# A two-layer attention and convolution trunk on one core: four edits around the end of attention jobs

## The chip, the cores and the metric

The kernel runs on one core of one Trainium2 chip. The metric is the device time of one execution in microseconds (us); of the kernel before, three runs are shown with their median. One further execution was profiled, and all rows below come from it. Its engines are named PE (TensorE matmul), PEld (weight load of PE, beside it), DVE (VectorE), ACT (ScalarE), POOL (GpSimd) and SP (SyncE, here only a queue that issues DMAs). Times in rows are counted from the start of the span.

## The reference, cut to what matters

Two layers; in each, 2048 latent tokens and 256 context tokens pass an input projection, eight-head attention, two convolution branches and an output projection:

```python
def one_block(qi):
    s = jnp.einsum('bqhd,bkhd->bhqk', qi, k).astype(jnp.float32) * sm_scale
    p = jax.nn.softmax(s, axis=-1).astype(v.dtype)
    return jnp.einsum('bhqk,bkhd->bqhd', p, v)
...
y = mixer_branches(parts, attn, ...)            # y_a = attn * silu(g_a), and two more branches
x_new = x + gate[:, None, :] * (y @ w_out[l])
```

All is float32. Latent queries see 256 + 2048 keys; context queries see the 256 context keys, and only in the first layer.

## The kernel before, in words

**Stages.** Per layer the program runs `tokens`, `features`, `attention` and `project`. In the profile the attention of layer 0 lies at about 815 to 1790 us, its projection at 1762 to about 1970, the attention of layer 1 at about 2640 to 3557, its projection from 3544 to the end.

**Attention jobs.** A job is one head and 512 queries; there are 32 per layer, in order of heads, and in layer 0 the last job of each head also carries 256 context queries. A job goes through its 18 key tiles in 9 pairs (one more pair for the context queries). For one pair PE makes two scores tiles `sc` in three matmuls each (L1074 to L1076), ACT takes the exponential twice, as `p` in float32 and `ph` in a reduced form (L1077, L1078), one `tensor_tensor` subtracts them to the rest `pl` (L1081), and one pair later PE multiplies `ph` and `pl` with the values into `po` (L1103, L1104). DVE adds `p` to the row sums `acc` in PSUM (L1088). Beside that PE computes for the next job all its scores once more as `pmax` (L986), whose maxima DVE reduces to `mx` (L987). `pmax` has two PSUM buffers (tag "b"), so PE waits there once DVE is two tiles late; `p` has four buffers.

**The end of a job** is `close` (L1109 to L1120, called by `flush` behind the products of the last pair): ACT copies `acc` to `accs` (L1108) and `po` to `o` (L1110), SP stores `o`, PE transposes `accs` in four pieces (L1116), DVE adds along the rows (L1118: `sm`), doubles the sums (L1119), and takes the reciprocal into `rinv` (L1120). The factor 2 makes up for the gate, which is stored at twice its value (as x times 1 + tanh(x/2)).

**The last job of a layer.** It has no next job, hence no `pmax` beside most of it. There DVE takes the subtraction L1081 of every odd pair (five instructions in layer 0, four in layer 1); POOL has all the others.

**Projection.** `project` splits each of eight weight blocks (128 x 1024) into `woh` (ACT, L191) and `wol` (DVE, L192) by way of one buffer `wraw`, and each block of 512 tokens into `yh` and `yl`. For the four parts k of attention output, `prepare_y` loads the two halves `yr` and `ylo` and the gate `yg`, spreads the reciprocals `rinv` over 128 columns in four small tiles `rr` (L1178), transposes these on PE into `prr` (L1179), and DVE makes sum, product and product (L1180 to L1182). Then PE has 24 matmuls per output tile (`pout`, L195 to L197). `rr` has three buffers. `prr` of the first block uses the PSUM tag "b" of `pmax`; weights 0 to 2, 3, and 4 to 7 lie in three pools whose memory comes free with tiles of attention.

**Order.** The framework orders each engine's instructions at build time by priority and a simulated timeline; on the chip every engine works its list in order. `attention` returns a mark: the priority at a given number of pairs (`AE`) before the end of the last job. What `project` issues under `start()` (weights 0 to 3 and the first block's `prepare_y`) gets the priority of that mark.

Of the kernel before, what the change touches and what calls it, by code (L numbers as in the profile page):

```python
# [9 lines left out]
F32 = mybir.dt.float32  # L10
F32R = mybir.dt.float32r
I32 = mybir.dt.int32
AF = mybir.ActivationFunctionType
ALU = mybir.AluOpType
# [4 lines left out]
P = 128  # L19
# [30 lines left out]
MV = 0  # L50
MD = 2
NE = 2
PV = 0
AE = 2
WM = (0,0,0,1,2,2,2,2)
SPV = 7
ZF = 4
# [28 lines left out]
def trunk(ctx: ExitStack, tc: tile.TileContext, ins, out):  # L86
    nc = tc.nc
    V, S, G, PE = nc.vector, nc.scalar, nc.gpsimd, nc.tensor

    def pool(stack, name, **kw):  # L90
        return stack.enter_context(tc.tile_pool(name=name, bufs=kw.pop("bufs", 1), **kw))
# [9 lines left out]
    rinv = [cst.tile([P, NTT, H], F32, name=f"rinv{l}") for l in range(DEPTH)]  # L101
# [838 lines left out]
    def attention(l, start):  # L940
# [3 lines left out]
        op = pool(es, f"Ao{l}", reuse_waits="tile", side="right")  # L944
# [4 lines left out]
        jobs = []  # L949
# [6 lines left out]
        scale = QK ** -0.5  # L956
# [3 lines left out]
        def load(h):  # L960
            K = hp[h % 2].tile([97, NTT, 2, P], F32R, tag="K", name="K")
            G.dma_start(K[0:NOPE], kn_d[l][h])
            G.dma_start(K[NOPE:97], kr_d[l][h])
            Q = hp[h % 2].tile([97, NTT, 2, P], F32R, tag="Q", name="Q")
            nq_ = (SEQ if last else NT) // P
            G.dma_start(Q[0:QK, :nq_], q_d[l][h, :, :nq_])
            Vt = vp.tile([P, NTT, P], F32R, tag=f"V{h % 2}", name="Vt")
            G.dma_start(Vt, v_d[l][h])
            kv[h] = (K, Vt, Q)
# [84 lines left out]
        for idx, job in enumerate(jobs):  # L1054
            h = job[0][0]
            if job[0][1] == (1024 if h else 512) and h + 1 < H:
                load(h + 1)
            pairs = [(j, it) for j in job for it in range(j[3], NTT, 2)]
            for pi, ((h, s, n, k0), kt0) in enumerate(pairs):
                if idx == len(jobs) - 1 and pi == len(pairs) - AE:  # L1060
                    mark = tc.cur_priority
                K, Vt, Q = kv[h]
                first, final = kt0 == k0, kt0 == NTT - 2
                if first:
                    po = psum("c", "po")
                    acc = psum("d", "acc")
                p = tp.tile([P, 2, 512], F32, tag="p", name="p", bufs=4)
                ph = tp.tile([P, 2, 512], F32R, tag="ph", name="ph", bufs=3)
                pl = tp.tile([P, 2, 512], F32R, tag="pl", name="pl", bufs=3)
                scs = []  # L1070
                for z in range(2):
                    kt, qt = kt0 + z, slice(s // P, (s + n) // P)
                    sc = psum("a", "sc")
                    PE.matmul(sc[:, :n], lhsT=K[0:97, kt, 0], rhs=Q[0:97, qt, 0], start=True, stop=False)  # L1074
                    PE.matmul(sc[:, :n], lhsT=K[0:QK, kt, 0], rhs=Q[0:QK, qt, 1], start=False, stop=False)  # L1075
                    PE.matmul(sc[:, :n], lhsT=K[0:QK, kt, 1], rhs=Q[0:QK, qt, 0], start=False, stop=True)  # L1076
                    S.activation(p[:, z, :n], sc[:, :n], AF.Exp, scale=scale)  # L1077
                    S.activation(ph[:, z, :n], sc[:, :n], AF.Exp, scale=scale)  # L1078

                by = V if idx == len(jobs) - 1 and pi % 2 and pi > PV else G  # L1080
                by.tensor_tensor(pl[:, :, :n], p[:, :, :n], ph[:, :, :n].bitcast(F32), op=ALU.subtract)  # L1081
                flush()

                for z in range(2):
                    if first and z == 0:
                        V.tensor_copy(acc[:, :n], p[:, 0, :n])
                    else:
                        V.tensor_tensor(acc[:, :n], acc[:, :n], p[:, z, :n], op=ALU.add)  # L1088
                for z in range(2):
                    at = pi + (z + 1) / 2 + LEAD  # L1090
                    if at <= len(pairs):
                        ahead(idx + 1, at / len(pairs))
                    else:
                        ahead(idx + 1, 1)
                        ahead(idx + 2, (at - len(pairs)) / len(pairs))
                if pi == len(pairs) // 2:
                    split_mods()
                if pi == len(pairs) - ME:
                    use_mods()

                def products(kt0=kt0, n=n, Vt=Vt, ph=ph, pl=pl, po=po, first=first, final=final):
                    for z in range(2):
                        PE.matmul(po[:, :n], lhsT=Vt[:, kt0 + z, :], rhs=ph[:, z, :n], start=first and z == 0, stop=False)  # L1103
                        PE.matmul(po[:, :n], lhsT=Vt[:, kt0 + z, :], rhs=pl[:, z, :n], start=False, stop=final and z == 1)  # L1104

                def close(h=h, s=s, n=n, po=po, acc=acc):
                    accs = op.tile([P, 512], F32, tag="o", name="accs", bufs=3)
                    S.copy(accs[:, :n], acc[:, :n])  # L1108
                    o = op.tile([P, 512], F32, tag="o", name="o", bufs=3)  # L1109
                    S.copy(o[:, :n], po[:, :n])  # L1110
                    nc.sync.dma_start(o_d[l][h, :, s : s + n], o[:, :n])

                    nq = n // P
                    px = psum("e", "psum_t")
                    for t in range(nq):
                        PE.transpose(out=px[:, t * P : (t + 1) * P], in_=accs[:, t * P : (t + 1) * P], identity=idn)  # L1116
                    sm = tp.tile([P, 4], F32, tag="sm", name="sm", bufs=2)
                    V.tensor_reduce(sm[:, :nq], px[:, :n].rearrange("p (t k) -> p t k", k=P), axis=AX.X, op=ALU.add)  # L1118
                    V.tensor_scalar(sm[:, :nq], sm[:, :nq], 2.0, None, op0=ALU.mult)  # L1119
                    V.reciprocal(rinv[l][:, s // P : s // P + nq, h], sm[:, :nq])  # L1120

                late.append(products)
                if final:
                    late.append(close)
        if not AE:
            mark = tc.cur_priority
# [8 lines left out]
    def project(l, start):  # L1135
# [3 lines left out]
        op = pool(es, f"Oo{l}", reuse_waits="tile", side="right")  # L1139
# [18 lines left out]
        def prepare_y(bi):  # L1158
            s, n = blocks[bi]
            where = (ap, bp)[bi % 2]  # L1160
            yh = where.tile([P, KD, 512], F32R, tag="yh", name="yh")[:, :, :n]
            yl = where.tile([P, KD, 512], F32R, tag="yl", name="yl")[:, :, :n]
            ys[bi] = (yh, yl)
            for k in order:
                r = rp.tile([P, 512], F32, tag="yr", name="yr", bufs=4)
                if k >= 4:
                    nc.sync.dma_start(r[:, :n], y_d[l][(k - 4) * P : (k - 3) * P, s : s + n])
                else:
                    lo = rp.tile([P, 512], F32, tag="ylo", name="ylo", bufs=2)
                    g = rp.tile([P, 512], F32, tag="yg", name="yg", bufs=2)  # L1170
                    for z in range(2):
                        nc.sync.dma_start(r[64 * z : 64 * z + 64, :n], o_d[l][2 * k + z, 0:64, s : s + n])
                        nc.sync.dma_start(lo[64 * z : 64 * z + 64, :n], o_d[l][2 * k + z, 64:128, s : s + n])
                    nc.sync.dma_start(g[:, :n], sga_d[l][k * P : (k + 1) * P, s : s + n])
                    px = psum("b" if bi == 0 else "cde"[k % 3], "prr")
                    for t in range(n // P):
                        rr = rp.tile([P, 2, 64], F32, tag="rr", name="rr", bufs=RR)
                        V.tensor_copy(rr, rinv[l][:, s // P + t, 2 * k : 2 * k + 2].unsqueeze(2).to_broadcast([P, 2, 64]))  # L1178
                        PE.transpose(out=px[:, t * P : (t + 1) * P], in_=rr.rearrange("p a b -> p (a b)"), identity=idn)  # L1179
                    V.tensor_tensor(r[:, :n], r[:, :n], lo[:, :n], op=ALU.add)  # L1180
                    V.tensor_tensor(r[:, :n], px[:, :n], r[:, :n], op=ALU.mult)
                    V.tensor_tensor(r[:, :n], r[:, :n], g[:, :n], op=ALU.mult)  # L1182
                split(yh[:, k, :n], yl[:, k, :n], r[:, :n], V if bi == 0 and (SPV & 4 and k < 4 or SPV & 8 and k >= 4) else None)
                yield
# [9 lines left out]
        for bi, (s, n) in enumerate(blocks):  # L1194
# [4 lines left out]
            acc = None if last else rp.tile([P, 512], F32, tag="acc", name="acc")  # L1199
# [114 lines left out]
```

## Time and profile before

| | |
|---|---|
| runs | 3740.6 us median of three (3739.18 to 3740.98) |
| profiled execution | 3738.87 us, span 3737.1 us |
| PE, PEld | 3543.0 us (95%), 2920.5 us (78%) |
| DVE | 3004.7 us (80%) |
| ACT, POOL | 2143.5 us (57%), 2324.0 us (62%) |
| mean granted clock of PE | 0.975 of full |

The span is read by stage. PE is busy for most of it in every stage, so what counts is where PE stands idle and where its granted clock is at 0.5 (1.2 GHz) in place of 1.0 (2.4 GHz), and which engine it waits for there.

### The profile page before, as it was taken

The page shows a single profiled execution, that of the slowest core. Times are in us where ns is not written, and L with a number is a line of the kernel's source. Part 1 is how long each engine was busy: PE and PEld are TensorE (multiplying, and loading weights), DVE is VectorE, ACT ScalarE, POOL GpSimd, SP SyncE. Part 2 cuts the span into 40 slices and gives each one's busy share as a digit, 9 for nine tenths or more (in the row PEclk, how much of TensorE's full clock was granted, in tenths as well). Part 3 has the DMA queues.
Part 4 walks back from the last instruction along what each step waited for, and adds up shares of the span by engine and source line. Part 5 has one row for each costly group of instructions (what it writes and reads, how often), then busy time and mean ns, then how long its engine had stood idle before and what let it go on. Part 6 is the DMA issues. An engine that isn't in the chain of part 4 may idle for free. (4 is left out here: it accounts for less than half of the span.)

```text
span 3737.1 us, 52826 instructions
## 1 busy us (share of the span) xinstructions
PE 3543.0 (95%) x17532; PEld 2920.5 (78%) x17532; DVE 3004.7 (80%) x5689; ACT 2143.5 (57%) x4192; POOL 2324.0 (62%) x1488
## 2 busy tenths in 40 slices
PE   7889999999999999988999989999999999998999
PEld 5787888887777787777788878887777777776777
DVE  6986886878888888899447878769998999999942
ACT  4665343247777777766335663433677777777610
POOL 4664444358888888875435654444687877877521
PEclk8899999999999999999999999999999999999999
DMA  7566334441333313312666773435222202222163
GB/s 216 171 187 200 88 104 118 109 128 48 85 80 78 78 36 77 79 58 59 220 218 212 216 214 102 117 101 129 77 69 61 45 22 61 58 58 76 40 197 114
DMA packets 394387, 411.48 MB, mean 110 GB/s; under 512 B 19168, under 2 KB 332128, under 8 KB 388960
## 3 DMA queue, kind: packets, MB, share of 16 engines
q1 hardware_dynamic: 387712, 333.87, 30.7%
q0 software_dynamic: 6400, 74.22, 8.8%
q8 instruction: 138, 2.26, 0.3%
q14 instruction: 137, 1.12, 0.1%
HBM read 266.72 MB, written 141.59 MB: 109 GB/s over the span
## 5 line engine op out<-in xcount | busy, mean ns | idle before, releaser
L1081 POOL TENSOR_TENSOR pl<-p,ph 128x1024 fp32r<-128x1024 f32 (+1 forms) x575 | 1365.1, 2391 | 322.5 <-ACT ph L1078 163.9
L987 DVE TENSOR_REDUCE mx<-pmax 128x1 fp32r<-128x512 f32 (+1 forms) x1296 | 794.8, 628 | 98.3 <-PE pmax L986 92.6
L1077 ACT ACTIVATE p<-sc 128x512 f32<-128x512 f32 x1168 | 708.6, 608 | 287.8 <-PE sc L1076 269.3
L1088 DVE TENSOR_TENSOR acc<-acc,p 128x512 f32<-128x512 f32 x1096 | 756.2, 690 | 45.6 <-ACT p L1077 20.2
L1078 ACT ACTIVATE ph<-sc 128x512 fp32r<-128x512 f32 x1168 | 698.2, 607 | 18.3 <-PE po L1103 13.3
L195 PE MATMUL pf<-hhf,wh 128*128 128x256 f32 (+1 forms) x1584 | 547.5, 347 | 14.1 <-ACT wh L191 7.0
L197 PE MATMUL pf<-hhf,wl 128*128 128x512 f32 (+1 forms) x1584 | 544.5, 345 | 5.6 <-POOL wl L192 5.4
L196 PE MATMUL pf<-hlf,wh 128*128 128x256 f32 (+1 forms) x1584 | 546.2, 345 | 0.0
L986 PE MATMUL pmax<-K,Q 96*128 96x512 f32 (+1 forms) x1296 | 474.3, 389 | 57.1 <-DVE mx L987 48.7
L1074 PE MATMUL sc<-Q,K 97*128 97x512 f32 x1168 | 478.8, 410 | 4.3 <-ACT Q L996 1.5
L1104 PE MATMUL po<-pl,Vt 128*128 128x512 f32 x1168 | 468.8, 402 | 5.6 <-DVE pl L1081 5.1
L1075 PE MATMUL sc<-Q,K 96*128 96x512 f32 x1168 | 467.3, 400 | 0.0
L1076 PE MATMUL sc<-Q,K 96*128 96x512 f32 x1168 | 465.0, 398 | 0.0
L1103 PE MATMUL po<-ph,Vt 128*128 128x512 f32 x1168 | 462.0, 396 | 0.7 <-DMA Vt<-v_d 0.7
L192 POOL TENSOR_TENSOR wl<-wraw,wh 128x1024 fp32r<-128x1024 f32 x104 | 254.3, 2446 | 284.7 <-ACT wh L191 267.2
L748 DVE SCALAR_TENSOR_TENSOR cacc<-z,hv,cacc 128x384 f32<-128x384 f32 (+5 forms) x780 | 403.6, 564 | 14.3 <-ACT cacc L743 11.2
L986 PEld LDWEIGHTS pmax<-K,Q 96*128 96x128 f32 x1296 | 246.2, 190 | 152.7 <-DVE mx L987 94.6
L195 PEld LDWEIGHTS pf<-hhf,wh 128*128 128x128 f32 x1584 | 302.7, 191 | 52.9 <-ACT wh L191 9.2
L197 PEld LDWEIGHTS pf<-hhf,wl 128*128 128x128 f32 x1584 | 301.8, 191 | 45.9 <-POOL wl L192 9.2
L196 PEld LDWEIGHTS pf<-hlf,wh 128*128 128x128 f32 x1584 | 303.0, 191 | 36.0 <-POOL hlf L192 0.2
L1074 PEld LDWEIGHTS sc<-Q,K 97*128 97x128 f32 x1168 | 223.6, 191 | 61.6 <-ACT ph L1078 9.6
L1104 PEld LDWEIGHTS po<-pl,Vt 128*128 128x128 f32 x1168 | 222.9, 191 | 56.8 <-DVE pl L1081 6.4
(259 smaller groups left out, 6304.1 us busy)
## 6 DMA issues: line engine op xcount, KB each, us to landing
wraw<-in_w_in SPq DMA_DIRECT2D x108, 512.0 KB
q_d<-sg SPq DMA_DIRECT2D x68, 384.0 KB
wm<-in_w_mod SPq DMA_DIRECT2D x46, 512.0 KB
v_d<-vs SPq DMA_DIRECT2D x36, 512.0 KB
kn_d<-sg SPq DMA_DIRECT2D x72, 256.0 KB
K<-kn_d POOLq DMA_DIRECT2D x16, 1152.0 KB, 8.5
Vt<-v_d POOLq DMA_DIRECT2D x16, 1152.0 KB, 14.0
o_d<-o SPq DMA_DIRECT2D x64, 256.0 KB
```

The costliest lines, as they stand in the source:

```text
L195: PE.matmul(out_, lhsT=ahi, rhs=bhi, start=first, stop=False)
L196: PE.matmul(out_, lhsT=ahi, rhs=blo, start=False, stop=False)
L197: PE.matmul(out_, lhsT=alo, rhs=bhi, start=False, stop=last)
L986: PE.matmul(pm[:, :w], lhsT=Q[0:QK, s // P + t, 0], rhs=K[0:QK, a // P : (a + w) // P, 0], start=True, stop=True)
L987: V.tensor_reduce(part[:, t, c : c + 1], pm[:, :w], axis=AX.X, op=ALU.max)
L1074: PE.matmul(sc[:, :n], lhsT=K[0:97, kt, 0], rhs=Q[0:97, qt, 0], start=True, stop=False)
L1075: PE.matmul(sc[:, :n], lhsT=K[0:QK, kt, 0], rhs=Q[0:QK, qt, 1], start=False, stop=False)
L1077: S.activation(p[:, z, :n], sc[:, :n], AF.Exp, scale=scale)
L1078: S.activation(ph[:, z, :n], sc[:, :n], AF.Exp, scale=scale)
L1081: by.tensor_tensor(pl[:, :, :n], p[:, :, :n], ph[:, :, :n].bitcast(F32), op=ALU.subtract)
L1088: V.tensor_tensor(acc[:, :n], acc[:, :n], p[:, z, :n], op=ALU.add)
L1104: PE.matmul(po[:, :n], lhsT=Vt[:, kt0 + z, :], rhs=pl[:, z, :n], start=False, stop=final and z == 1)
```

## The change

Four edits. The doubling L1119 on DVE is dropped; ACT's copy L1108 becomes an activation of kind Copy with scale 2.0. The subtraction L1081 is always POOL's, in the last jobs too, and its constant `PV` goes. The mark is set 8 pairs before the end of the last job instead of 2 (`AE`). The spreading copies `rr` (L1178) are ACT's instead of DVE's, in all blocks of both layers.

```diff
-PV = 0
-AE = 2
+AE = 8
...
-                by = V if idx == len(jobs) - 1 and pi % 2 and pi > PV else G
-                by.tensor_tensor(pl[:, :, :n], p[:, :, :n], ph[:, :, :n].bitcast(F32), op=ALU.subtract)
+                G.tensor_tensor(pl[:, :, :n], p[:, :, :n], ph[:, :, :n].bitcast(F32), op=ALU.subtract)
...
-                    S.copy(accs[:, :n], acc[:, :n])
+                    S.activation(accs[:, :n], acc[:, :n], AF.Copy, scale=2.0)
...
-                    V.tensor_scalar(sm[:, :nq], sm[:, :nq], 2.0, None, op0=ALU.mult)
...
-                        V.tensor_copy(rr, rinv[l][:, s // P + t, 2 * k : 2 * k + 2].unsqueeze(2).to_broadcast([P, 2, 64]))
+                        S.copy(rr, rinv[l][:, s // P + t, 2 * k : 2 * k + 2].unsqueeze(2).to_broadcast([P, 2, 64]))
```

## Rows read from the trace of the kernel before

**Rows 1.** Busy time by stage: stretch, length, busy by engine (instructions), PEclk, DMA share, GB/s.

```profile
core 0: us, PE busy (x) PEld busy (x) DVE busy (x) ACT busy (x) POOL busy (x), PEclk, DMA share, GB/s
815.00:1625.00 810.00, 795.68 (x3864) 637.94 (x3863) 714.78 (x1303) 618.11 (x1156) 690.03 (x314) 0.98 0.30 72
1625.00:1800.00 175.00, 146.72 (x662) 114.04 (x661) 155.91 (x239) 105.73 (x200) 97.06 (x45) 0.93 0.28 85
...
2690.00:3405.00 715.00, 698.90 (x3058) 549.95 (x3057) 647.83 (x1089) 533.62 (x1009) 568.66 (x261) 1.00 0.23 54
3405.00:3570.00 165.00, 149.18 (x625) 114.47 (x624) 144.95 (x222) 103.69 (x192) 99.84 (x45) 0.95 0.29 84
```

**Rows 2.** Waits of PE, 820 to 1625 us: total us, times, longest.

```profile
PE pmax L986 <- DVE mx L987: 10.2, 10, 1.4
PE pm L217 <- DVE mx L987: 2.4, 1, 2.4
```

**Rows 3.** Waits of PE, 1625 to 1800 us.

```profile
PE pmax L986 <- DVE mx L987: 12.6, 3, 6.8
PE prr L1179 <- DVE rr L1178: 9.2, 6, 5.6
PE po L1104 <- DVE pl L1081: 3.2, 2, 1.7
PE pm L217 <- DVE mx L987: 2.2, 1, 2.2
```

**Rows 4.** Waits of PE, 2690 to 3405 us.

```profile
PE pmax L986 <- DVE mx L987: 13.1, 39, 0.7
```

**Rows 5.** Waits of PE, 3405 to 3570 us.

```profile
PE pmax L986 <- DVE mx L987: 6.6, 5, 4.8
PE prr L1179 <- DVE rr L1178: 2.2, 2, 1.2
PE po L1104 <- DVE pl L1081: 1.9, 1, 1.9
```

**Rows 6.** The instructions of line 1119: durations in ns (least, median, longest).

```profile
L1119 DVE TENSOR_SCALAR sm<-sm x72: 157/1284/6940, 836.4 to 3562.8; 128x4 f32<-128x4 f32 x64, 128x2 f32<-128x2 f32 x8
```

**Rows 7.** Timeline from 1050 to 1055 us: start, us, engine, line [idle before <- releaser].

```profile
1050.74 2.69 DVE L1119 TENSOR_SCALAR sm<-sm 128x4 f32<-128x4 f32 x1
1051.03 2.37 POOL L192 TENSOR_TENSOR wml<-wm,wmh 128x1024 fp32r<-128x1024 f32 x1
...
1053.35 0.68 DVE L987 TENSOR_REDUCE mx<-pmax 128x1 fp32r<-128x512 f32 x1
...
1054.08 0.38 PE L986 MATMUL pmax<-K,Q 96*128 96x256 f32 x1 [1.43 <-DVE mx L987]
```

**Rows 8.** Timeline of PE in layer 1, from 3117 to 3122 us.

```profile
3120.77 0.50 PE L986 MATMUL pmax<-K,Q 96*128 96x512 f32 x1 [0.42 <-DVE mx L987]
```

**Rows 9.** Busy time in three stretches at the lower clock (columns as in rows 1).

```profile
1055.10:1058.50 3.40, 3.40 (x11) 2.75 (x10) 2.48 (x7) 2.44 (x5) 1.62 (x3) 0.50 1.09 181
...
1642.20:1649.00 6.80, 3.91 (x10) 3.14 (x11) 6.80 (x11) 1.18 (x3) 2.14 (x2) 0.50 0.03 8
3427.30:3434.10 6.80, 3.77 (x9) 2.99 (x10) 6.66 (x10) 1.65 (x3) 2.79 (x3) 0.50 0.32 81
```

**Rows 10.** The instructions of `rr` and `accs` by tile: durations in ns.

```profile
L1178 DVE COPY rr<-rinv x136: 193/219/2394, 1626.2 to 3683.9; 128x128 f32<-128x128 f32 x136
...
L1108 ACT COPY accs<-acc x72: 375/587/602, 833.2 to 3553.5; 128x512 f32<-128x512 f32 x64, 128x256 f32<-128x256 f32 x8
```

**Rows 11.** Timeline of ACT, one row at the start of layer 0's projection.

```profile
1782.87 1.05 ACT L191 CAST woh<-wraw 128x1024 fp32r<-128x1024 f32 x1 [4.87 <-DMA wraw<-in_w_out]
```

**Rows 12.** Line 1222 in layer 0's projection: busy us, mean ns, idle before it.

```profile
L1222 ACT ACTIVATE xg<-xo,gain 128x512 f32<-128x512 f32 (+1 forms) x38 | 25.8, 679 | 33.2 <-POOL acc L1221 32.5 <-ACT xg L1220 0.7
```

**Rows 13.** The instructions that write `pl`, by tile: durations in ns.

```profile
L1081 POOL TENSOR_TENSOR pl<-p,ph x575: 1266/2400/3066, 810.8 to 3544.7; 128x1024 fp32r<-128x1024 f32 x189, 128x512 fp32r<-128x512 f32 x3
L1081 DVE TENSOR_TENSOR pl<-p,ph x9: 675/1216/2802, 1744.8 to 3542.8; 128x1024 fp32r<-128x1024 f32 x8, 128x512 fp32r<-128x512 f32 x1
```

**Rows 14.** Timeline of DVE, one row before layer 0's last job.

```profile
1715.41 8.63 DVE L192 TENSOR_TENSOR wol<-wraw,woh 128x1024 fp32r<-128x1024 f32 x1
```

## Prediction

> **What bounds the kernel now.** I read the stages first, then PE's waits in each, then the timeline around the longest. PE is the engine that sets the end: in the two steady stretches of attention it is busy for 795.7 of 810 us and 698.9 of 715 us, and at the two seams where attention becomes projection for 146.7 of 175 and 149.2 of 165 [rows 1]. So what can be won lies in PE's idle time and in stretches at the lower clock, and the seams have most of it for their length. The waits of PE name one engine: DVE. In layer 0's attention PE waits 10.2 + 2.4 us for `mx` [rows 2], at its seam 12.6 + 2.2 us for `mx`, 9.2 for `rr` and 3.2 for `pl` [rows 3]; in layer 1 it is 13.1 us [rows 4] and at the seam 6.6, 2.2 and 1.9 [rows 5]. That makes 63.6 us.
>
> Why is DVE late? The doubling L1119 works on 128 x 4 numbers and takes 157 ns at best, but 1284 ns in the median and 6.94 us at worst [rows 6]. The timeline shows what it does meanwhile: it starts at 1050.74 and ends at 1053.43, POOL's subtraction started at 1051.03 and ends at 1053.40; the next `mx` starts only then, and PE, which needs that buffer for its next `pmax`, has stood idle for 1.43 us [rows 7]. The small instruction is held until POOL's is done, and everything behind it on DVE's list is held too. `rr`, also a copy inside SBUF, shows the same: 219 ns in the median, 2394 at worst [rows 10]. By the Trainium skill (SBUF — State Buffer, "Who interferes with whom") copies and tensor_scalar on DVE can lock the port pair shared with GpSimd, and DVE instructions with two SBUF inputs contend with GpSimd's reads as well; the trace agrees, with an end 0.03 us behind POOL's.
>
> **Part 1, the doubling.** 72 instructions go from DVE; ACT's copy becomes an activation with a constant scale, on the same elements, which I cost at nothing (ACT has 192 us free of 810 in the first stretch [rows 1]; if it cost 0.1 us on the path, 72 x 0.1 = 7 us, a bound). What PE gets back, stage by stage:
> - Layer 0, steady: the 2.4 us wait [rows 2] stands behind a doubling, and six waits like the 1.43 us one [rows 7], one per head: 2.4 + 6 x 1.43 = 11.0. After four of them PE works 3.4 us at clock 0.50, as from 1055.1 [rows 9]; that work would take half as long at 1.00: 4 x 1.7 = 6.8. Together **17.8**.
> - Layer 0, seam: the longest wait, 6.8 us [rows 3], stands behind the 6.94 us doubling [rows 6], and 3.91 us of work at clock 0.50 follow [rows 9], costing 2.0. The longer of the `pl` waits, 1.7 us [rows 3], has a doubling just ahead of it on DVE's list too. **10.5**.
> - Layer 1, steady: 19 of the 39 waits in [rows 4] stand right behind a doubling, as the one of 0.42 us in [rows 8] (0.25 to 0.72 each): 19 x 0.43 = **8.2**. Of the other 20 (4.9 us) I take half, **2.4**, since DVE gains 1 to 2 us in each job.
> - Layer 1, seam: 4.8 us [rows 5], and 3.77 us of work at 0.50 [rows 9], costing 1.9: **6.7**.
>
> Sum 45.6. These instructions can't be late again, as they are gone; `mx` and `acc`, which follow, have an operand in PSUM.
>
> **Part 2, spreading on ACT.** Of the waits for `rr`, 9.2 + 2.2 + 2.2 us with the `pm` wait behind two held copies [rows 3, 5], all could go (13.6). The 5.6 us one I count half: it falls where the weights are split, and ACT stands 4.87 us for a weight's DMA just there [rows 11], so on ACT `rr` may wait as well. That leaves 8.0 + 2.8 = **10.8** won. Cost on ACT: `accs` takes 375 ns for 256 columns and 587 for 512 [rows 10], so 128 columns are about 270 ns (estimate on that line); 16 in each last job make 4.3 us, beside 61 and 71 us of ACT's idle time at the seams [rows 1]. In layer 0's projection ACT's list has waits of its own: 33.2 us before 38 instructions of L1222 [rows 12], 0.87 us each; an `rr` behind one makes PE's `prr` late. 16 groups of `rr` there: 0 to 14 us; I take **2** lost, near the low end, because three `rr` buffers let ACT work ahead.
>
> **Part 3, POOL alone.** Nine subtractions go from 1.22 us on DVE to 2.40 on POOL [rows 13]. If all lie on PE's path that costs 9 x 1.18 = 10.7; if DVE's were late anyway, the remaining `pl` waits (3.2 + 1.9 - 1.7 = 3.4) [rows 3, 5] are won. I take **4** lost: POOL is idle 78 and 65 us at the seams [rows 1], so it has the time, but a pair of the last job then needs 2.4 us of POOL beside some ten matmuls of PE, and little slack is left. The Trainium skill (Perfetto Trace Analysis, "Optimizing GPSIMD Operations") advises to prefer other engines where possible, and speaks against this part; by it the full 10.7 would be paid, and the sum below would come out 6.7 us higher.
>
> **Part 4, the mark 8 pairs ahead.** I cost it at nothing. The first `rr` already start at 1626 [rows 10], more than four jobs before the end, and what holds the rest is memory, not priority: `prr` needs the PSUM tag of `pmax`, the later weights need the pools of the last head. Its bounds: some of the waits of parts 1 and 2 counted half could go (5 us), or it brings DVE's splits to where POOL runs without a pause (the slow rival below).
>
> **Sum.** 45.6 + 10.8 - 2 - 4 = 50.4. The profiled execution took 3738.9 us (span 3737.1), so 3688.5; it lies 1.7 us under the median of the runs, so I forecast **3690** for the median.
>
> **Rivals.** (a) *The seams keep their loss.* Only the steady stretches change, 17.8 + 8.2 = 26, because DVE's weight split, which was held 8.63 us [rows 14], and the other two-input instructions of `prepare_y` stall PE in place of what went: 3738.9 + 1.7 - 26 = 3715. For it: there are 20 such instructions per layer and nothing of the change touches them; against: in the last job no `pmax` waits for DVE. (b) *More.* All 63.6 us of waits go and 11 of clock with them: 3666. Against: that 8.63 us split is among them. (c) *Slower: preparation under a POOL that never pauses.* With POOL on every pair and the splits and products of `prepare_y` moved forward, each of the 20 per layer (weight splits, `yl`, L1180, L1182) is held for one subtraction, 2.40 us [rows 13]: 40 x 2.4 = 96 us of DVE time. Less the 45.6 of part 1, that is 3740.6 + 96 - 46 = 3791 if all reaches PE. It decides once `acc` falls more than four pairs behind, since then ACT finds no free `p` buffer. Against: DVE's own `pl`, two SBUF inputs as well, took 1216 ns in the median and 2802 at worst [rows 13], so most got through beside POOL. The Trainium skill's page named above (SBUF — State Buffer, same section) would have two-input instructions wait like this. (d) *The change does nothing here:* ordering at build time moves another port-locking instruction into each gap: 3740.
>
> **How the numbers follow.** Forecast case (3675 to 3705) 0.62; (a) 0.18; (b) 0.09; (c) 0.06; (d) 0.05. The range takes in (b) and (a) with part 3 at its full price: **3664 to 3726**. A measurement of this kernel can tell 0.2% (7.5 us) from no change: faster by more than that has the forecast, (a), (b), together 0.89; within it 0.05; slower 0.06.
>
> **What would show it.** No L1119; in the steady stretches PE's waits for `mx` fall below 2 us in layer 0 and to about 3 in layer 1, and the four short stretches at 0.50 between 1055 and 1410 are gone. PE's waits for `rr` become waits for ACT, a few us in all. `pl` in the last jobs is POOL's alone, with PE waiting for it some us. I am wrong in size if the waits at the seams stay (DVE instructions with two inputs of over 2 us there), and in kind if PE's idle time in the steady stretches stays with another releaser.

## The result, and the profile after

The changed kernel takes 3695.91 us (median of four runs, 3688.82 to 3697.99) against 3739.89; its ratio to before is 0.9888, with a 95% interval of 0.9876 to 0.9900. In a second set of runs it came to 0.9889 (0.9869 to 0.9910). The forecast was 3690, with a range of 3664 to 3726. The profiled execution took 3695.0 us, span 3693.2: 43.9 us less span than before. Lines have moved up by one to four: the sums `yr` + `ylo` (L1180 before) are L1176, `pmax` is L985, `rr` L1174.

Busy time by stage, the stretches of [rows 1] moved to where the changed kernel is in the same work (stretch, length, busy time by engine with instructions, clock, DMA share, GB/s):

```profile
815.00:1607.00 792.00, 786.76 (x3875) 633.02 (x3875) 687.98 (x1276) 618.32 (x1158) 690.13 (x315) 1.00 0.31 76
1607.00:1775.00 168.00, 152.27 (x686) 118.94 (x685) 133.23 (x200) 110.41 (x227) 111.30 (x51) 0.94 0.31 94
2662.00:3362.00 700.00, 692.36 (x3055) 550.88 (x3054) 614.85 (x1062) 529.40 (x1008) 566.62 (x260) 1.00 0.24 55
3362.00:3527.00 165.00, 150.19 (x622) 115.95 (x621) 129.86 (x191) 107.11 (x213) 109.75 (x49) 0.94 0.30 85
```

The steady stretches are shorter by 18 and 15 us at about the same number of matmuls, and PE's idle time in them fell from 14.3 and 16.1 us to 5.2 and 7.6. In layer 1 PE's busy time fell too, from 698.9 to 692.4 us; the account of the prediction below says why. The seam of layer 0 has become shorter by some 7 us, that of layer 1 (165 us, 15 us idle) has not changed.

PE's waits in nearly the same four stretches (from 820, 1610, 2660 and 3360 us), in this order (total, times, longest; compare [rows 2 to 5]):

```profile
PE sc L1073 <- ACT ph L1077: 2.3, 1, 2.3
PE pmax L985 <- DVE mx L986: 1.6, 4, 0.6
...
PE pmax L985 <- DVE mx L986: 6.5, 2, 6.4
PE sc L1073 <- ACT ph L1077: 3.9, 2, 3.1
PE prr L1175 <- ACT rr L1174: 2.8, 1, 2.8
...
PE pmax L985 <- DVE mx L986: 4.7, 19, 0.4
...
PE pmax L985 <- DVE mx L986: 7.2, 5, 5.0
PE sc L1073 <- ACT ph L1077: 3.1, 1, 3.1
```

In the steady stretches the waits for `mx` fell from 10.2 and 13.1 us to 1.6 and 4.7. At the seams the longest waits for `mx` are still there: 6.4 us where it was 6.8, 5.0 where it was 4.8. The timeline shows who stands in the doubling's place (first DVE's row at layer 0's seam, then DVE, POOL and PE at layer 1's; start, us):

```profile
1624.42 6.87 DVE L1176 TENSOR_TENSOR yr<-yr,ylo 128x512 f32<-128x512 f32 x1 [1.43 <-DMA yr<-o_d]
...
3386.46 5.36 DVE L1176 TENSOR_TENSOR yr<-yr,ylo 128x512 f32<-128x512 f32 x1 [1.46 <-DMA yr<-o_d]
...
3381.90 9.37 POOL L1078 TENSOR_TENSOR pl<-p,ph 128x1024 fp32r<-128x1024 f32 x4
...
3392.21 0.79 PE L985 MATMUL pmax<-K,Q 96*128 96x512 f32 x1 [5.03 <-DVE mx L986]
```

The doubling is gone, and the next DVE instruction that can be held is the sum of `yr` and `ylo`, with two inputs in SBUF. POOL runs four subtractions without a gap, from 3381.90 to 3391.27; the sum, issued at 3386.46, is done at 3391.82, only after the last of them, and `mx` and PE wait behind it as before.

A second hold at each seam reaches PE by another way. The waits for `ph` have grown from 0.4 to 3.9 us in layer 0 and from 1.0 to 3.1 in layer 1, and the long one in each, 3.1 us, comes about like this (DVE, POOL, ACT, PE in layer 1):

```profile
3491.15 2.63 DVE L1178 TENSOR_TENSOR yr<-yr,yg 128x512 f32<-128x512 f32 x1
...
3490.86 2.37 POOL L1078 TENSOR_TENSOR pl<-p,ph 128x1024 fp32r<-128x1024 f32 x1
...
3493.81 0.62 ACT L190 CAST yh<-yr 128x512 fp32r<-128x512 f32 x1 [3.97 <-DVE yr L1178]
...
3495.47 0.50 PE L1073 MATMUL sc<-Q,K 97*128 97x512 f32 x1 [3.09 <-ACT ph L1077]
```

DVE's product is held by POOL's subtraction; `yh`, next on ACT's list, waits 3.97 us for it; the exponentials stand behind `yh`, and PE waits for them.

ACT's new work, by tile (durations in ns, least, median, longest):

```profile
L1105 ACT ACTIVATE accs<-acc x72: 389/598/610, 837.9 to 3502.5; 128x512 f32<-128x512 f32 x64, 128x256 f32<-128x256 f32 x8
...
L1174 ACT COPY rr<-rinv x136: 279/297/512, 1610.8 to 3639.7; 128x128 f32<-128x128 f32 x136
```

The copy that doubles costs 11 ns more than the plain one [rows 10], and an `rr` takes 297 ns on ACT, 512 at most, against 219 ns and up to 2394 on DVE.

### The profile page after: what moved, and what is told of

Same layout as the page of the kernel before. It is cut to its first block, busy times and chain, and to the rows that moved or that the text cites. A ratio compares the mean times of both kernels' runs of the same rounds, so it can differ in the third digit from the quotient of the medians.

```text
span 3693.2 us, 52810 instructions
## 1 busy us (share of the span) xinstructions
PE 3529.8 (96%) x17532; PEld 2916.9 (79%) x17532; DVE 2888.8 (78%) x5472; ACT 2166.7 (59%) x4328; POOL 2341.6 (63%) x1497
## 5 line engine op out<-in xcount | busy, mean ns | idle before, releaser
L1078 POOL TENSOR_TENSOR pl<-p,ph 128x1024 fp32r<-128x1024 f32 (+1 forms) x584 | 1387.2, 2397 | 276.2 <-ACT ph L1077 110.4
L1077 ACT ACTIVATE ph<-sc 128x512 fp32r<-128x512 f32 x1168 | 703.8, 612 | 20.1 <-PE po L1100 16.2
L194 PE MATMUL pf<-hhf,wh 128*128 128x256 f32 (+1 forms) x1584 | 549.3, 348 | 18.2 <-ACT tg L867 8.4
L985 PE MATMUL pmax<-K,Q 96*128 96x512 f32 (+1 forms) x1296 | 465.0, 386 | 34.8 <-DVE mx L986 26.8
L747 DVE SCALAR_TENSOR_TENSOR cacc<-z,hv,cacc 128x384 f32<-128x384 f32 (+5 forms) x780 | 403.0, 561 | 14.3 <-ACT cacc L742 11.2
L985 PEld LDWEIGHTS pmax<-K,Q 96*128 96x128 f32 x1296 | 245.3, 190 | 116.9 <-DVE mx L986 58.6
L1075 PEld LDWEIGHTS sc<-Q,K 96*128 96x128 f32 x1168 | 224.5, 192 | 51.5
## 6 DMA issues: line engine op xcount, KB each, us to landing
Vt<-v_d POOLq DMA_DIRECT2D x16, 1152.0 KB, 14.8
```

The source lines that it names most:

```text
L194: PE.matmul(out_, lhsT=ahi, rhs=bhi, start=first, stop=False)
L985: PE.matmul(pm[:, :w], lhsT=Q[0:QK, s // P + t, 0], rhs=K[0:QK, a // P : (a + w) // P, 0], start=True, stop=True)
L1078: G.tensor_tensor(pl[:, :, :n], p[:, :, :n], ph[:, :, :n].bitcast(F32), op=ALU.subtract)
```

## The experiments

To compare traces by stage, I take the times at which ACT makes `accs` of the same job, and the last `pout` of layer 0; in the kernel before the stages so cut run from 936 to 1627, to 1994, and from 2698 to 3415 us, to the end. Differences of a stage's length to before, in us, each from one profiled execution; "rest" is everything outside:

| kernel | ratio to before (95%) | steady, layer 0 | seam and projection, layer 0 | steady, layer 1 | seam and projection, layer 1 | rest |
|---|---|---|---|---|---|---|
| changed kernel | 0.9888 (0.9876 to 0.9900) | -17.8 | -14.0 | -14.7 | -0.8 | +3.4 |
| changed kernel again (b0) | 0.9889 (0.9869 to 0.9910) | -17.7 | -14.3 | -16.3 | -4.2 | +2.2 |
| e1, doubling on ACT alone | 0.9903 (0.9884 to 0.9922) | -18.2 | +3.2 | -16.0 | -3.8 | -0.5 |
| e2, doubling as a sum on DVE | 0.9896 (0.9874 to 0.9918) | -18.1 | +2.6 | -16.5 | +2.1 | +1.6 |
| e3, `rr` on ACT alone | 0.9990 (0.9977 to 1.0003) | +4.8 | -5.9 | -1.9 | -2.1 | -1.7 |
| e4, POOL alone | 0.9991 (0.9979 to 1.0002) | +4.4 | -6.4 | -1.6 | +4.1 | -1.5 |
| a2, changed but `rr` on DVE | 0.9902 (0.9884 to 0.9921) | -18.1 | -5.3 | -14.4 | -0.2 | +4.7 |
| a3, changed but odd `pl` on DVE | 0.9865 (0.9846 to 0.9884) | -17.8 | -11.4 | -16.2 | -2.1 | +2.9 |
| a4, changed, sum on POOL | 0.9852 (0.9832 to 0.9871) | -17.8 | -21.2 | -16.3 | +0.9 | +1.9 |
| a5, changed, all `yl` of block 0 on DVE | 0.9897 (0.9881 to 0.9913) | -17.7 | -7.3 | -14.6 | +0.3 | -1.1 |
| b1, a4 and weights 0 to 3 on POOL | 0.9824 (0.9805 to 0.9843) | -17.7 | -21.3 | -16.3 | -11.5 | -1.4 |
| b2, a4 and odd `pl` on DVE | 0.9850 (0.9831 to 0.9870) | -17.7 | -21.2 | -16.3 | -2.5 | -0.3 |
| b3, b1 and odd `pl` on DVE | 0.9829 (0.9808 to 0.9850) | -17.8 | -19.8 | -14.8 | -10.4 | -1.5 |

Single executions of one kernel differ by up to 0.4% from their median, and the two traces of the changed kernel by up to 3.4 us in a stage, so a stage of one trace is read for where a wait stands, and the ratio for what it is worth.

**The mark needed no run.** With 2 or with 8 pairs, in the kernel before and in the changed one, the program built is the same: PE, DVE, ACT, POOL and SP have the same instructions in the same order. That part of the change does nothing.

**e1: the doubling alone.**

```diff
-                    S.copy(accs[:, :n], acc[:, :n])
+                    S.activation(accs[:, :n], acc[:, :n], AF.Copy, scale=2.0)
-                    V.tensor_scalar(sm[:, :nq], sm[:, :nq], 2.0, None, op0=ALU.mult)
```

Expected: 

> The kernel before with the doubling alone moved into ACT's copy; all else as before. Theory L (DVE is held by POOL, and at the two seams the hold passes on to the next DVE instruction with two SBUF inputs, the sum of yr and ylo): the steady stretches give 17.8 + 10.6 us, the long holds of 6.9 and 5.9 us at the seams come back under another line, so some 28 to 33 us under the kernel before, 3707 to 3712. Theory S (the seams gain as the prediction had it, 45.6 us): 3694. Theory N (what the whole change won came from the other parts): within 10 us of before.

Measured 0.9903, 36 us. That is most of what the whole change gives, and by theory L's stages: 18.2 and 16.0 us in the steady stretches, next to nothing at the seams. There DVE's sum stands in for the doubling (DVE, POOL, PE at layer 1's seam of e1):

```profile
3397.95 8.19 DVE L1180 TENSOR_TENSOR yr<-yr,ylo 128x512 f32<-128x512 f32 x2 [1.47 <-DMA yr<-o_d]
...
3393.27 11.71 POOL L1081 TENSOR_TENSOR pl<-p,ph 128x1024 fp32r<-128x1024 f32 x5
...
3407.13 0.79 PE L986 MATMUL pmax<-K,Q 96*128 96x512 f32 x1 [6.80 <-DVE mx L987]
```

**e2: the doubling stays on DVE, as another instruction.**

```diff
-                    V.tensor_scalar(sm[:, :nq], sm[:, :nq], 2.0, None, op0=ALU.mult)
+                    V.tensor_reduce(s2x[:, :nq], sm[:, :nq].unsqueeze(2).to_broadcast([P, nq, 2]), axis=AX.X, op=ALU.add)
```

Expected: 

> The kernel before with the doubling still on DVE, in the same place and as many instructions, but as a sum over two views of the same number (a tensor_reduce, like L990, which took some 165 ns beside POOL). Theory L: what costs is being held by POOL, not the instruction: every doubling takes under 0.2 us, and the time is that of e1 within 6 us. Rival (the instruction itself, or its place on DVE's list and the order at build time, costs): the time stays within 8 us of the kernel before, 3732 to 3748.

Measured 0.9896, the same as e1 within the intervals. DVE has as many instructions as before, PE's list is that of before but for a few places, and the 72 doublings take:

```profile
L1119 DVE TENSOR_REDUCE s2x<-sm x72: 143/150/163, 840.2 to 3532.8; 128x4 f32<-128x8 f32 x64, 128x2 f32<-128x4 f32 x8
```

163 ns at most, where it was 6940 [rows 6]. So it wasn't one more instruction on DVE's list, nor its place there, nor the order at build time: what the doubling cost was the hold by POOL, which this form of it doesn't meet. The Trainium skill (SBUF — State Buffer, "Who interferes with whom") states that on trn2 tensor_reduce never contends for the shared ports while tensor_scalar and copies can; these 72 durations agree.

**e3: `rr` on ACT alone.** In the kernel before, `V.tensor_copy(rr, ...)` becomes `S.copy(rr, ...)`.

Expected: 

> The kernel before with only the rr copies moved to ACT. By the prediction 10.8 - 2 = 8.8 us faster, 3731. Rival: at the seams PE waits for ACT's rr, and for the doublings that remain, in place of DVE's rr, so within 4 us of before; or slower by up to 14 us if rr stands behind ACT's own waits in layer 0's projection.

Measured 0.9990, 3.7 us, which can't be told from no change; the 8.8 us forecast lie just outside the interval.

**e4: POOL alone.** In the kernel before, `by = G` in place of the choice between V and G.

Expected: 

> The kernel before with POOL taking every subtraction of the last jobs. By the prediction 4 us slower, 3744, between 3.4 us faster and 10.7 us slower. Rival: with DVE's two-input instructions held longer by a POOL that runs without a pause, over 10 us slower.

Measured 0.9991: neither 4 us slower nor over 10; it can't be told from no change.

**a2 and a3: undoing one part of the changed kernel.** The copies `rr` go back to `V.tensor_copy`; the odd subtractions of the last jobs go back to V.

Expected of a2: 

> The changed kernel with the rr copies back on DVE. If rr on ACT pays only once the doublings are gone (stage by stage the changed kernel gained some 14 us between the last jobs and the end of layer 0's projection that the doubling alone did not): 6 to 12 us slower than the changed kernel, 3702 to 3708, ratio 0.990 to 0.992. If rr on ACT is worth nothing: within 4 us, 0.988 to 0.990.

Measured 0.9902: 5 us slower than the changed kernel, with overlapping intervals. The stages put it at layer 0's seam and projection, 5.3 us gained instead of 14.0. a3 beside e1 is the same comparison without POOL alone: 14 us by the ratio (0.9865 and 0.9903), 14.6 at the same stage. So `rr` on ACT is worth some 5 to 14 us if the doublings are gone; the stages say so more clearly than the ratios.

Expected of a3: 

> The changed kernel with every odd subtraction of the last jobs back on DVE. By the prediction's step POOL alone cost 4 us, so 4 us faster than the changed kernel, 3692. By the run of that part alone (0.9991) it cost nothing: 0 to 4 us slower.

Measured 0.9865, 8 us faster, its interval just overlapping that of the changed kernel. But b2 below undoes the same part and gains nothing, a2 beside e1 shows nothing, and e4 had the other sign. The traces show one cost: PE's waits for `ph` by way of ACT, 3.9 and 3.1 us in the changed kernel (5.1 and 3.1 in b0), come to 0.2 us in a3 and to nothing in a2. As long as the sum stays on DVE, they come only where `rr` on ACT and POOL alone meet. By the times, what POOL alone costs stays below what these runs tell.

**a4: taking away the instruction that is held now.**

```diff
-                    V.tensor_tensor(r[:, :n], r[:, :n], lo[:, :n], op=ALU.add)
+                    (G if bi == 0 else V).tensor_tensor(r[:, :n], r[:, :n], lo[:, :n], op=ALU.add)
```

Expected: 

> The changed kernel with the sum of yr and ylo of the first block (four in each layer) on POOL instead of DVE. The changed kernel lies at 0.9888 of before, 3696. Theory L (at each seam DVE's first instruction with two SBUF inputs, this sum, is held by a run of POOL subtractions, 6.9 and 5.4 us): PE's waits of 6.4 and 5.0 us and the work at the lower clock behind them (7.4 and 5.8 us, half of it lost) go, 18 us less some POOL time: 3680 to 3688, ratio 0.984 to 0.986. Rival H (the hold passes on once more, to the weight split or the products): within 5 us of the changed kernel.

Measured 0.9852, 13 us under the changed kernel, with intervals apart: theory L by the ratio, and faster than both kernels. But the stages split it: layer 0's seam gained another 7 us, layer 1's gained nothing. There the rival came true (DVE, POOL, PE):

```profile
3376.98 10.16 DVE L191 TENSOR_TENSOR wol<-wraw,woh 128x1024 fp32r<-128x1024 f32 x1
...
3371.88 4.76 POOL L1078 TENSOR_TENSOR pl<-p,ph 128x1024 fp32r<-128x1024 f32 x2
3376.61 2.53 POOL L1176 TENSOR_TENSOR yr<-yr,ylo 128x512 f32<-128x512 f32 x2
3379.11 6.95 POOL L1078 TENSOR_TENSOR pl<-p,ph 128x1024 fp32r<-128x1024 f32 x3
...
3387.80 0.80 PE L985 MATMUL pmax<-K,Q 96*128 96x512 f32 x1 [7.34 <-DVE mx L986]
```

The hold has passed on a second time, to the weight split, next on DVE's list with two SBUF inputs; POOL runs from 3371.88 to 3386.06 without a pause, and the split ends 1.08 us after that.

**a5: a shorter run of POOL.** The four `yl` that POOL makes just ahead of the run go to DVE (`SPV = 15`).

Expected: 

> The changed kernel with the four first yl of the first block on DVE instead of POOL (5.6 us less of POOL's unbroken run at each seam, four more two-input instructions on DVE). Theory L: POOL's run at each seam is shorter, so the sum of yr and ylo is held some 5 us less, but the yl can be held themselves: 0 to 12 us faster than the changed kernel, 3684 to 3696. Rival (holds depend on two-input instructions alone, not on POOL's run): slower by up to 10 us.

Measured 0.9897, no change. The holds of the sum got shorter (at most 2.9 us), but in layer 0 a weight split was held 8.7 us instead. Making POOL's run shorter by moving work to DVE won nothing here.

**b0 to b3: following the hold.** b0 is the changed kernel again. b1 is a4 with the lower part of weights 0 to 3 on POOL (`SPV = 6`), b2 is a4 with the odd subtractions of the last jobs on DVE, b3 has both.

Expected of b0: 

> The changed kernel itself, unaltered, beside the three below, so that they are compared on one chip: ratio 0.9888 as before, 0.987 to 0.990.

Expected of b1: 

> The sum of yr and ylo of the first block on POOL, and the lower part of weights 0 to 3 on POOL too, so that no DVE instruction with two SBUF inputs stands between the last pmax tiles. Theory L (with the sum on POOL the hold passed on to the weight split, 10.2 us in layer 1, with PE waiting 7.3 us): that wait and half of the slow work behind it go, 5 to 10 us under the run with the sum alone, ratio 0.982 to 0.984. Rival P (POOL, with 9.6 us more per seam, becomes what the pairs wait for): not under the run with the sum alone, 0.985 or more, with PE waiting for pl.

Expected of b2: 

> The sum of yr and ylo of the first block on POOL, and every odd subtraction of the last jobs on DVE again. If POOL alone costs what undoing it showed (0.9865 against 0.9888, 8 us), 4 to 9 us under the run with the sum alone, ratio 0.983 to 0.984. If it costs nothing, 0.985 to 0.986.

Expected of b3: 

> Both: the sum and the lower part of weights 0 to 3 on POOL, the odd subtractions of the last jobs on DVE. If both pay and add up, 0.979 to 0.982; if only one does, as that one.

Measured 0.9889, 0.9824, 0.9850 and 0.9829. b1 came out as theory L had it; b2 shows no cost of POOL alone, and b3 is as b1. The intervals of b1 and a4 overlap a little, but layer 1's seam tells them apart: 11.5 and 10.4 us gained in b1 and b3, nothing to 2.5 in a4 and b2. b1 is the fastest, 3672.8 us beside the changed kernel's 3700.4 in the same set, 28 us. Its waits at layer 0's seam (first three) and layer 1's (the others):

```profile
PE sc L1073 <- ACT ph L1077: 4.4, 4, 2.3
PE prr L1175 <- ACT rr L1174: 3.0, 2, 1.8
...
PE pmax L985 <- DVE mx L986: 0.2, 1, 0.2
...
PE pout L194 <- DVE xo L1206: 7.2, 1, 7.2
...
PE pmax L985 <- DVE mx L986: 0.5, 2, 0.3
```

Hardly any wait for `mx` is left, though eight two-input splits (four in each layer) went to POOL, which takes 2.4 us for one where DVE takes 1.2. What is last now at layer 1's seam is another thing: `xo`, for which DVE itself waits 6.8 us for a load.

## Why the prediction was right, and where not

The forecast of 50.4 us gained met 43.9 in the profile. By its steps:

- **The doubling in the steady stretches, right in mechanism, small in size.** Layer 0: 17.8 forecast, 17.8 measured, 18.2 and 18.1 in e1 and e2. That they are equal is chance: the forecast holds the 2.4 us wait, which lies at 841 us, ahead of the measured stage, and near it the changed kernel has a new wait of 2.3 us, for ACT's `ph`. For the stage itself the forecast was 15.4. Layer 1: 8.2 + 2.4 = 10.6 forecast, 14.7 measured (14.4 to 16.5 over the runs without the doubling). The waits for `mx` fell by 8.4, about as counted; the other 6 us stand in no row of waits. They are busy time of PE, and the trace of before shows where it comes from, at the wait of [rows 8]:

```profile
3119.72 0.40 PE L1076 MATMUL sc<-Q,K 96*128 96x512 f32 x1
3119.95 0.40 PE L986 MATMUL pmax<-K,Q 96*128 96x512 f32 x1
3120.77 0.50 PE L986 MATMUL pmax<-K,Q 96*128 96x512 f32 x1 [0.42 <-DVE mx L987]
3121.11 0.39 PE L1074 MATMUL sc<-Q,K 97*128 97x512 f32 x1
```

Elsewhere such matmuls start 0.23 us apart and overlap; here the starts are 0.82 and 0.34 us apart. The wait costs 0.70 us, and only 0.42 of it is idle time. With 39 waits before and 19 after, 20 x 0.28 = 5.6 us (an estimate from this one) are most of the 6. So the term was too small because it priced a wait at its idle time alone.

- **The doubling at the seams, wrong: 10.5 + 6.7 forecast, next to nothing measured.** The step that failed is the sentence "These instructions can't be late again, as they are gone; `mx` and `acc`, which follow, have an operand in PSUM." Not only these follow. `mx` and `acc` were indeed never held (0.70 us at most). But the sum of `yr` and `ylo` followed, and was held in the doubling's stead for 6.9 and 5.4 us; e1 and e2 show the same with the doubling's change alone. The prediction's own sign of being wrong in size, waits at the seams that stay behind two-input instructions of over 2 us, is what came. Rival (a) had named these instructions, at 0.18, and its mechanism was the right one at the seams; its price was wrong, since the rest of layer 0's seam did gain.
- **`rr` on ACT, right in size, but not by itself.** 10.8 - 2 forecast; by a2 8.7 in the stages and some 5 by the ratio, by a3 beside e1 some 14. That the parts add up, as the sum has it, isn't shown: with the doublings still there the same edit gave 3.7 us (e3), no more than noise. PE's waits for `rr` and for the `pm` behind it, 13.6 us in all before, came down to 2.8 at layer 0's seam and 1.1 at the start of layer 1's projection. The one of 5.6 us, counted half, became one of 2.8. The loss feared in layer 0's projection isn't seen: PE waits for no `rr` there after 1775 us. What ACT's list did cost is the 3.1 us wait for `ph` at each seam, behind `yh`, which the prediction didn't have. (ACT's idle time at layer 0's seam is 69 us by [rows 1], not 71; nothing hangs on it.)
- **POOL alone, not settled.** 4 us of cost forecast; 3 us gained alone, 8 lost by a3, none by b2 or by a2 beside e1. The rule of the Trainium skill (Perfetto Trace Analysis, "Optimizing GPSIMD Operations") that speaks against it would have made it 10.7; e4, at 0.9991 with an upper end of 1.0002, shows no such cost.
- **The mark, right.** Nothing, as the program built is the same. Whether for the reason given, memory and not priority, was not tried.
- **Rival (c), slower, did not come.** Two-input instructions are held, but in the changed kernel one long hold per layer reached PE by way of `mx` and one of 2.6 us by way of ACT's `yh`; the other holds of 2 to 3 us (the products and `yl` of `prepare_y`) mostly delay only what has time.

That the sum came out near is in part luck. Of the 17 us that the seams kept, 4 came back as layer 1's steady stretch gave more than was counted, and 4 more as POOL alone showed no such cost in the ratios. The rest, some 3 us, is less than two traces of the changed kernel differ by (b0's span is 6.5 us shorter).

## What to carry to other kernels

Count a DVE instruction that POOL can hold at up to the length of POOL's unbroken run, not by its own size, and before crediting its removal look for the next instruction on DVE's list with two SBUF inputs, or a copy or scaling inside SBUF: it takes over the hold. The way out in this kernel was to have none of them on DVE's list between the instructions that PE waits for: on ACT, as a reduce, or on POOL itself, even where POOL needs twice the time. Work that goes to ACT must not stand there behind something that waits for DVE. And price a wait of PE by the starts of its matmuls, not by the idle time alone.

## What had not been expected of the hardware

A hold need not be over with POOL's current instruction. With POOL's work back to back, DVE waited through the rest of the run: 5.36 us in a run of four subtractions, 8.19 us in one of five (two sums, in e1), 10.16 us in a4. In the six long holds of layer 0's steady part the run was over after 2.7 us, so one subtraction looked like the unit; but [rows 7] have the doubling on from 1050.74 and the POOL instruction that holds it only from 1051.03.

It is not always so. In the second trace of the changed kernel, b0, the same sum meets the same four subtractions at layer 1's seam and gets in after the third (a row each of DVE, POOL, PE):

```profile
3383.97 2.58 DVE L1176 TENSOR_TENSOR yr<-yr,ylo 128x512 f32<-128x512 f32 x1 [1.93 <-DMA yr<-o_d]
3378.95 9.83 POOL L1078 TENSOR_TENSOR pl<-p,ph 128x1024 fp32r<-128x1024 f32 x4
3386.94 0.80 PE L985 MATMUL pmax<-K,Q 96*128 96x512 f32 x1 [2.73 <-DVE mx L986]
```

The sum ends at 3386.55, POOL's run only at 3388.78. The hold is 2.58 us instead of 5.36 and PE's wait 2.7 instead of 5.0. What decides at the end of a POOL instruction whether DVE gets in is not shown here.

The lower clock behind the same wait isn't certain. In the profile of before, PE stood idle six times for 1.42 to 1.44 us in layer 0's steady stretch, and the clock was at 0.50 after four of them; in e3, with the same six waits at 1.41 to 1.43 us, it fell after all six. The 4.8 us more that e3 shows in that stage are in keeping with that.
